# Down projection of a ConvFFN: low parts of weight operands by accumulating DMAs instead of subtractions

## The chip, the cores and the metric

One core of a Trainium2 chip runs the whole block as one program. The time is device microseconds of one execution, given as the median of several runs. Three runs of the kernel before took 1481.59, 1489.31 and 1491.31 us: median 1489.31. The profile shows one execution, whose span from the first to the last instruction is 1485.7 us. In it the granted TensorE clock was 0.992 on the mean.

Engine names as in the profile: PE is TensorE's matmul (PEld its weight load), DVE VectorE, ACT ScalarE, POOL GpSimd, SP SyncE, which here only issues DMAs. Each engine works through its own queue in order. A DMA issue that has to wait holds up all that stands behind it in that queue.

## The reference

```python
def _conv_ffn(xn, w_up, conv_w, conv_b, w_down):
    hid = xn @ w_up
    hp = jnp.pad(hid, ((0, 0), (CONV_WIDTH - 1, 0), (0, 0)))
    conv = conv_b + sum(hp[:, j:j + seq_len] * conv_w[j] for j in range(CONV_WIDTH))
    val, gate = jnp.split(conv, 2, axis=-1)
    return (jax.nn.silu(gate) * val) @ w_down
...
    h = h + _conv_ffn(rmsnorm(h, norm_ffn_g), w_ffn_up, ffn_conv_w, ffn_conv_b, w_ffn_down)
    h = rmsnorm(h, norm_final_g)
    return h[:, N_META:]
```

Ahead of this stand a normalization, a forgetting attention beside a state-space model, and an output projection. The sizes: 1024 tokens and 16 meta tokens, width 1024, hidden width 2816, everything float32. The change touches only the last matrix product, the 1024x2816 by 2816x1024 down projection `@ w_down`, whose result is added to `h` and normalized.

## The kernel before

**Two-term operands.** Every float32 matrix operand is split into a high part `hi` (the value cast to fp32r, TensorE's reduced form of float32) and a low part `lo = x - hi`. A product is three matmuls: hi by hi, hi by lo, lo by hi (lines 1365, 1366, 1367 for the down projection: `ah` is the high part of the activation, `bh` and `bl` the high and the low part of the weight).

**Seven products.** The down projection is a Strassen-like scheme: both matrices are cut into 2x2 blocks, and seven products p = 0 to 6 of sums of blocks replace eight. `ORDER` takes them as 0, 4, 1, 2, 5, 3, 6. The hidden width is cut into 11 pairs of 128-row blocks, j = 0 to 10, in four groups: j = 0, 1; 2 to 4; 5 to 7; 8 to 10. A product of a group is 4 token tiles by 2 or 3 values of j by 3 matmuls of 128x128 by 128x512, gathered in four PSUM banks. Products 4, 5, 6 go on in the banks of products 0, 1, 3 (`JOINS`). Each time a bank is complete, DVE (ACT for some of the first group) adds it to the running sums in SBUF (line 1375 and lines 1370, 1373); that is called the eviction here. PE can't write on in a joined bank before its eviction has read it.

**Operand forms.** For each (group, product, j), `forms` (line 1289) makes one slot of four 128x512 tiles: activation hi and lo, weight hi and lo. There are 77 of them, numbered here in the order of the program, n = 0 to 13 in the first group, 14 to 34 in the second, and so on. For one form:

- SP loads the weight block `b_` (256 KB) into a buffer `wr` (8 buffers, line 1293): for products 0, 4 and 6 it is a block of `w_dn` itself, for 1, 2, 3 and 5 a sum of blocks that earlier DMAs have put into DRAM tensors `t_d`.
- POOL makes the activation sums in place (lines 1298 to 1304) from tiles `ar` that SP loads from `a_d`.
- ACT casts the activation and the weight to hi (line 1310).
- Both lo parts are subtractions, `split_lo` (line 129): on POOL for products 0, 4 and 5, on DVE for 1, 2, 3 and 6.

**Slots.** There are 14: four `op` tiles, eight in what `xhi` and `xlo` held before, and two more `op` tiles. Form n uses slot n modulo 14 (from the fifth on), so a slot is refilled as soon as the product that used it last has ended; `prepare` (line 1406) makes forms as far ahead as slots are free. The trace names the slots only as `op`, `xhi` and `xlo`.

**Order of the work.** The program is written in the order of `prepare` and `product`, and a scheduler of the framework then orders each engine's queue by a timing model of its own, so a changed instruction can also move its neighbours.

**The other way to make a low part**, already in the kernel, is used in the mixer's gate weights and the output projection (`lo_by_dma`, line 133): ACT writes -hi into the lo tile (line 135), then POOL issues a DMA that reads the same source block from DRAM a second time and adds it into the lo tile (line 136).

Of the kernel before, what the change touches and what calls it, by code (L numbers as in the profile page):

```python
# [19 lines left out]
P = 128  # L20
# [30 lines left out]
def block_kernel(ctx, tc, x, meta, g1, x0t, g1t, w_q, w_k, w_v, w_f, w_u, w_g, b_f, w_ao, lam_d, bw_d, cw_d,  # L51
# [5 lines left out]
    V, S, GP, PE, SY = nc.vector, nc.scalar, nc.gpsimd, nc.tensor, nc.sync  # L57
# [52 lines left out]
    t_d = {p: dp.tile([DFF // 2, 512], F, name=f"t_d{p}") for p in (1, 2, 3, 5)}  # L110
# [13 lines left out]
    def after(inst, first):  # L124
        tc.add_manual_dep(inst.ins, first.ins.name, mybir.DependencyInfo(
            mybir.DependencyClass.NoSync, mybir.DependencyReason.DATA), reason="order")

    def split_lo(eng, out_, src, hi):
        return eng.tensor_tensor(out_, src, hi.bitcast(F), ALU.subtract)  # L129
# [3 lines left out]
    def lo_by_dma(lo, hi, src):  # L133

        S.activation(lo, hi.bitcast(F), AF.Copy, scale=-1.0)
        GP.dma_start(lo, src.bitcast(R), accum_op=ALU.add)
# [784 lines left out]
    own_w = {0: (0, 0), 4: (1, 0), 6: (1, 1)}  # L921
# [277 lines left out]
    def w_block(k, h_, j):  # L1199
        c0 = P * (2 * j + k)  # L1200
        return w_dn[c0:c0 + P, 512 * h_:512 * h_ + 512]
# [76 lines left out]
    def behind(ld, j):  # L1278
        if h_load and j in groups[1]:
            after(ld, h_load[-1])  # L1280
# [9 lines left out]
    def forms(p, j):  # L1290
        r = pairs[j]
        b_ = down1.tile([P, 512], F, tag="w", name="wr", bufs=8)
        behind(SY.dma_start(b_, w_block(*own_w[p], j) if p in own_w else t_d[p][P * j:P * j + P]), j)

        a11, a21, a12, a22 = (r[k, h_] for k in range(2) for h_ in range(2))
        sub, add = ALU.subtract, ALU.add
        if p == 1:
            GP.tensor_tensor(a11, a11, a21, sub)
        elif p == 2:
            GP.tensor_tensor(a11, a22, a11, add)  # L1300
        elif p == 3:
            GP.tensor_tensor(a21, a22, a21, sub)
        elif p == 6:
            GP.tensor_tensor(a11, a11, a12, sub)
        slot = ops[n_op[0] % len(ops)]
        n_op[0] += 1
        a_ = (a11, a11, a11, a21, a12, a22, a11)[p]
        eng = GP if p in (0, 4, 5) else V
        for q, src in ((0, a_), (2, b_)):
            hi = S.copy(slot[q], src)  # L1310
            if first_copy and j < 2 and p >= 5:
                after(hi, first_copy[1])
            cut = split_lo(eng, slot[q + 1], src, slot[q])
            if first_add and eng is V and j < 2 and p > 2:
                after(cut, first_add[1 if p == 3 else 3])
        return slot
# [88 lines left out]
    def prepare():  # L1405

        while len(ready) < (len(items) if first_add else 3) and room[0] >= len(groups[items[len(ready)][0]]):
            g, p = items[len(ready)]
            room[0] -= len(groups[g])
            if p == 0:  # L1410
                for j in groups[g]:
                    load_pair(j)
            ready[g, p] = [forms(p, j) for j in groups[g]]
# [4 lines left out]
    for p in ORDER[:2]:  # L1418
        room[0] -= 2
        ready[0, p] = [forms(p, j) for j in groups[0]]  # L1420
# [416 lines left out]
```

## Time and profile before

| what | value |
|---|---|
| runs | 1481.59, 1489.31, 1491.31 us |
| median of the runs | 1489.31 us |
| span of the profiled execution | 1485.7 us |
| what lies around the span, taken as median less span | 3.6 us |
| down projection on PE, first to last matmul | about 1257.1 to 1477.8 us of the span |
| DMA load of a weight block `wr` from `t_d`, 256 KB, issue to landing | 2.8 us (median of 44) |
| the same from `w_dn` | 3.8 us (median of 33) |

The time of the profiled execution isn't listed apart from its span; the three runs lie between 4.1 us under and 5.6 us over that span, so the profiled one is an ordinary execution and the median is taken for its time.

How to read the lines shown further down. A line of the groups view has: source line, engine, operation, output<-inputs, shape, count | busy us in total, mean ns of one | idle time of the engine just before them, and what ended it. A line of the timeline has: start us, length us, engine, line, operation, output<-inputs, count of merged instructions [idle time before <- releaser]. A line of the windows view has: the stretch, its length, then the busy time of PE, PEld, DVE, ACT and POOL with the number of instructions, the granted PE clock, the mean busy share of the 16 DMA engines, and GB/s. A line of the waits view says who waited for whom: total us, times, the longest. Line 129 is the helper of all subtractions: `op<-wr,op` is a weight's low part, `op<-ar,op` an activation's.

### The profile page before, as it was taken

What the parts mean: (1) busy time and instruction counts of PE and PEld (TensorE: products, weight loads), DVE (VectorE), ACT (ScalarE), POOL (GpSimd) and SP (SyncE); (2) the same over time, 40 slices, a digit from 0 to 9 for tenths busy, and PEclk for the clock granted to TensorE, in tenths of its full rate; (3) what the DMA queues carried; (4) which work ended last, traced back from release to release, by engine and by line L of the source; (5) the groups of instructions that cost most, each with busy time, mean ns of one, the idle gap of its engine ahead of it and who ended that gap; (6) DMA issues with size and microseconds to landing.
All of it is one profiled execution on the core that took longest, in us unless ns stands there. A gap on an engine that the chain in (4) does not pass through costs nothing. (4 is left out here: it accounts for less than half of the span.)

```text
span 1485.7 us, 26584 instructions
## 1 busy us (share of the span) xinstructions
PE 1440.4 (97%) x9712; PEld 1358.8 (91%) x9712; DVE 1071.4 (72%) x2173; ACT 712.2 (48%) x1384; POOL 742.1 (50%) x850
## 2 busy tenths in 40 slices
PE   7999997999999999999999999999999999998997
PEld 7989996998899999999888999999999999777886
DVE  6879648881566676647468987888877776788785
ACT  6434675541555665543546534444444445543433
POOL 1311125752456465524863144455544426789766
PEclk9999999999999999999999999999999999999999
DMA  6366571551127342047885135676653215765513
GB/s 246 86 157 157 128 163 50 177 160 43 48 79 178 93 111 90 26 148 256 257 158 185 57 109 141 178 199 188 174 143 100 84 57 180 286 203 148 168 40 114
DMA packets 91032, 206.72 MB, mean 139 GB/s; under 512 B 14651, under 2 KB 25531, under 8 KB 90517
## 3 DMA queue, kind: packets, MB, share of 16 engines
q1 hardware_dynamic: 69380, 159.73, 32.9%
q0 software_dynamic: 15296, 34.63, 13.2%
q10 hardware_dynamic: 6224, 10.65, 1.9%
q8 instruction: 77, 1.26, 0.3%
q14 instruction: 55, 0.44, 0.1%
HBM read 165.90 MB, written 69.35 MB: 158 GB/s over the span
## 5 line engine op out<-in xcount | busy, mean ns | idle before, releaser
L159 PE MATMUL mm<-xhi,whi 128*128 128x342 f32 (+2 forms) x488 | 159.4, 327 | 1.0 <-DVE q L129 1.0
L161 PE MATMUL mm<-xhi,wlo 128*128 128x342 f32 (+2 forms) x488 | 158.3, 325 | 0.0
L160 PE MATMUL mm<-xlo,whi 128*128 128x342 f32 (+2 forms) x488 | 157.7, 324 | 0.0
L1079 POOL TENSOR_TENSOR ov<-ov,og 128x1024 f32<-128x1024 f32 x21 | 51.1, 2434 | 125.6 <-ACT og L1078 121.7
L129 DVE TENSOR_TENSOR sw<-sf,sw 128x512 fp32r<-128x512 f32 x72 | 66.6, 925 | 50.0 <-ACT sw L1070 49.8
L1070 ACT CAST sw<-sf 128x512 fp32r<-128x512 f32 x72 | 44.9, 624 | 106.2 <-POOL sf L1196 74.5
L159 PEld LDWEIGHTS mm<-xhi,whi 128*128 128x128 f32 x488 | 91.9, 188 | 2.1 <-PE sp L714 0.8
L161 PEld LDWEIGHTS mm<-xhi,wlo 128*128 128x128 f32 x488 | 91.8, 188 | 0.3
L160 PEld LDWEIGHTS mm<-xlo,whi 128*128 128x128 f32 x488 | 91.9, 188 | 0.2
L763 ACT CAST th<-tp 128x256 fp32r<-128x256 f32 (+3 forms) x120 | 56.2, 472 | 62.5 <-PE tp L756 30.1
L129 DVE TENSOR_TENSOR tl<-tp,th 128x256 fp32r<-128x256 f32 (+3 forms) x120 | 65.2, 547 | 25.1 <-ACT th L763 23.7
L1196 POOL TENSOR_TENSOR sf<-raw,sf 128x512 f32<-128x512 f32 x36 | 59.1, 1641 | 44.8 <-DVE sw L129 44.7
L1196 POOL TENSOR_TENSOR sf<-raw 128x512 f32<-128x512 f32 x36 | 48.0, 1332 | 66.9 <-DMA raw<-in_w_up_dram 35.9
L221 PE MATMUL mm<-xhi,sw 128*128 128x258 f32 (+1 forms) x288 | 81.0, 281 | 0.0
L219 PE MATMUL mm<-xhi,sw 128*128 128x258 f32 (+1 forms) x288 | 80.8, 281 | 0.0
L220 PE MATMUL mm<-xlo,sw 128*128 128x258 f32 (+1 forms) x288 | 80.7, 280 | 0.0
L728 POOL TENSOR_SCALAR pt<-pt,nm 128x144 f32<-128x144 f32 (+4 forms) x72 | 51.8, 731 | 48.5 <-DVE nm L727 47.5
L1248 DVE SCALAR_TENSOR_TENSOR ov<-hv,cwt,ov 128x1024 f32<-128x1024 f32 x36 | 72.5, 2014 | 0.1
L1070 ACT CAST sw<-raw 128x512 fp32r<-128x512 f32 x70 | 43.0, 621 | 53.3 <-PE sp L221 25.5
L726 ACT ACTIVATE pt<-pt,nm 128x144 f32<-128x144 f32 (+4 forms) x72 | 52.9, 735 | 26.1 <-DVE nm L725 25.7
L719 DVE CUSTOM_DVE_ANT_0 pt<-sp,fb 128x328 f32<-128x328 f32 (+8 forms) x112 | 46.4, 430 | 20.0 <-PE sp L714 11.1
L756 PE MATMUL tp<-ident,pt 128*128 128x128 f32 (+1 forms) x360 | 58.3, 270 | 0.1
(708 smaller groups left out, 5702.1 us busy)
## 6 DMA issues: line engine op xcount, KB each, us to landing
raw<-in_w_up_dram SPq DMA_DIRECT2D x44, 512.0 KB, 3.6
t_d<-in_w_dn_dram POOLq DMA_DIRECT2D x44, 256.0 KB, 7.0
ar<-a_d SPq DMA_DIRECT2D x44, 256.0 KB, 5.1
wr<-t_d SPq DMA_DIRECT2D x44, 256.0 KB, 2.8
a_d<-ov SPq DMA_DIRECT2D x21, 512.0 KB, 2.6
wr<-in_w_dn_dram SPq DMA_DIRECT2D x33, 256.0 KB, 3.8
t_d<-in_w_dn_dram SPq DMA_DIRECT2D x22, 256.0 KB, 4.2
t_d<-t_d SPq DMA_DIRECT2D x22, 256.0 KB, 4.7
```

The source lines that it names most:

```text
L129: return eng.tensor_tensor(out_, src, hi.bitcast(F), ALU.subtract)
L159: yield PE.matmul(ps, whi[:, i, :], ahi[:, i], start=(i == 0), stop=False)
L160: yield PE.matmul(ps, whi[:, i, :], alo[:, i], start=False, stop=False)
L161: yield PE.matmul(ps, wlo[:, i, :], ahi[:, i], start=False, stop=(i == k - 1))
L219: PE.matmul(ps, a[0][:, i], bh, start=(i == 0 and not joins), stop=False, skip_group_check=True)
L220: PE.matmul(ps, a[0][:, i], bl, start=False, stop=False, skip_group_check=True)
L221: PE.matmul(ps, a[1][:, i], bh, start=False, stop=(i == kh - 1), skip_group_check=True)
L756: PE.transpose(tp[:kn, o:o + n], p_[:n, k0:k0 + kn], ident[:n, :n])
L763: S.copy(th[:kn, z:tw], tp[:kn, z:tw])
L1070: S.copy(hi, src)
L1196: sums.append(GP.tensor_tensor(f_, a, b, op))
L1248: V.scalar_tensor_tensor(out=o, in0=h_[:, j:SEQ + j], scalar=cwc(j, m), in1=o, op0=ALU.mult, op1=ALU.add)
```

## The change

In `forms`, the low part of the weight is no longer a subtraction for j >= 2, that is for the second to fourth group: `lo_by_dma` makes it. For j = 0 and 1 all stays, as do the low parts of the activations. The source of the weight block gets a name, so that both the load and the accumulating DMA can use it.

```diff
     def forms(p, j):
         r = pairs[j]
         b_ = down1.tile([P, 512], F, tag="w", name="wr", bufs=8)
-        behind(SY.dma_start(b_, w_block(*own_w[p], j) if p in own_w else t_d[p][P * j:P * j + P]), j)
+        b_src = w_block(*own_w[p], j) if p in own_w else t_d[p][P * j:P * j + P]
+        behind(SY.dma_start(b_, b_src), j)
...
         eng = GP if p in (0, 4, 5) else V
         for q, src in ((0, a_), (2, b_)):
             hi = S.copy(slot[q], src)
+            if q and j >= 2:
+                lo_by_dma(slot[3], slot[2], b_src)
+                continue
             if first_copy and j < 2 and p >= 5:
                 after(hi, first_copy[1])
             cut = split_lo(eng, slot[q + 1], src, slot[q])
```

The function that it calls, as it stands in both kernels:

```python
    def lo_by_dma(lo, hi, src):

        S.activation(lo, hi.bitcast(F), AF.Copy, scale=-1.0)
        GP.dma_start(lo, src.bitcast(R), accum_op=ALU.add)
```

The build shows that no queue is reordered ahead of the down projection. In the queues of the down projection 36 subtractions leave DVE and 27 leave POOL; 63 copies with scale -1 join ACT's queue, and 63 DMA issues join POOL's. On PE the number of matmuls stays, and around the change from the first to the second group their order is another.

## The prediction

> **What bounds the kernel now.** I read the page's head first, then the windows view over the down projection, then PE's waits there.
>
> ```profile
> span 1485.7 us, 26584 instructions
> PE 1440.4 (97%) x9712; PEld 1358.8 (91%) x9712; DVE 1071.4 (72%) x2173; ACT 712.2 (48%) x1384; POOL 742.1 (50%) x850
> ...
> 1257.00:1478.00 221.00, 212.43 (x935) 173.55 (x933) 175.10 (x214) 96.96 (x190) 176.46 (x127) 1.00 0.49 156
> 1265.00:1335.00 70.00, 67.91 (x297) 55.29 (x297) 54.26 (x61) 36.99 (x69) 58.57 (x39) 1.00 0.75 252
> 1265.00:1445.00 180.00, 173.57 (x758) 141.43 (x758) 146.31 (x169) 81.51 (x154) 148.34 (x103) 1.00 0.56 174
> ```
>
> PE is the bound: in the 221 us of the down projection it is busy for 212.43 us at full clock, so it stands idle for 8.57 us. The change doesn't touch a matmul, so 8.57 us is all that it can win in this stretch. DVE and POOL are busy for 175 us each and ACT for 97; none is the bound, but each can hold PE up. The idle time, from the waits of PE in the same stage:
>
> ```profile
> PE mm L1365 <- ACT xlo L1310: 3.0, 1, 3.0
> PE tp L1365 <- DVE hs L1375: 2.7, 2, 2.0
> PE mm L1365 <- DVE hs L1375: 1.1, 1, 1.1
> PE sp L1367 <- POOL op L129: 0.9, 1, 0.9
> PE sp L1365 <- DVE hs L1375: 0.6, 1, 0.6
> ```
>
> The 1.1 us (a load of `hs`) and 2.0 of the 2.7 us (the last product) have nothing to do with weights. The 3.0 us ended at 1368.6; here is DVE ahead of it:
>
> ```profile
> 1357.52 3.48 DVE L129 TENSOR_TENSOR op<-wr,op 128x512 fp32r<-128x512 f32 x2
> 1360.92 2.33 DVE L129 TENSOR_TENSOR op<-ar,op 128x512 fp32r<-128x512 f32 x1
> ...
> 1366.58 0.68 DVE L129 TENSOR_TENSOR xhi<-wr,xhi 128x512 fp32r<-128x512 f32 x1
> 1367.18 0.68 DVE L1375 TENSOR_TENSOR hs<-hs,tp 128x512 f32<-128x512 f32 x1
> 1367.77 1.87 DVE L1375 TENSOR_TENSOR u<-u,mm 128x512 f32<-128x512 f32 x3
> ```
>
> The eviction of the joined `mm` bank starts at 1367.77, and one of it takes 0.6 us: PE goes on at 1368.6. The wait is put down to ACT, but the eviction fits it better; it stood behind three weight subtractions.
>
> **What the change removes.** The groups of the stage, weight subtractions on both engines:
>
> ```profile
> L129 POOL TENSOR_TENSOR op<-wr,op 128x512 fp32r<-128x512 f32 x19 | 27.6, 1465 | 0.0
> L129 DVE TENSOR_TENSOR op<-wr,op 128x512 fp32r<-128x512 f32 x15 | 22.7, 1520 | 0.0
> L129 DVE TENSOR_TENSOR xhi<-wr,xhi 128x512 fp32r<-128x512 f32 x15 | 16.9, 1130 | 0.0
> L129 DVE TENSOR_TENSOR xlo<-wr,xlo 128x512 fp32r<-128x512 f32 x14 | 15.9, 1144 | 0.0
> L129 POOL TENSOR_TENSOR xhi<-wr,xhi 128x512 fp32r<-128x512 f32 x8 | 12.6, 1578 | 0.0
> L129 POOL TENSOR_TENSOR xlo<-wr,xlo 128x512 fp32r<-128x512 f32 x6 | 8.6, 1439 | 0.0
> ```
>
> DVE: 44 in 55.5 us, 1.26 us each; 8 of the first group stay, 36 go: 45 us. POOL: 33 in 48.8 us, 1.48 us each; 6 stay, 27 go: 40 us. Neither is on PE's path as such. What DVE's 45 us are worth is the evictions that stand behind them: 3.0 + 0.6 + 0.7 us = 4.3 us. Bounds: 0 (another activation subtraction takes the place in the queue) and 4.3; I take 4.3, because in the changed order of DVE the evictions of a bank follow each other with fewer subtractions between them. The 0.9 us of PE on POOL goes as well, since that place is priced anew below.
>
> **What it adds.** The same construction stands in the output projection; its rows:
>
> ```profile
> L135 ACT ACTIVATE op<-op x8: 615/625/636, 719.6 to 755.1; 128x512 fp32r<-128x512 f32 x8
> ...
> L136 POOL DMA_DIRECT2D op<-to_d x4: 877/1293/1795, 724.1 to 725.8; - x4
> ...
> DMA to landing us min/median/max: 4.1/6.8/12.1
> ...
> op<-to_d POOLq DMA_DIRECT2D x4, 256.0 KB, 9.9
> ...
> 724.08 3.54 POOL L136 DMA_DIRECT2D op<-to_d  x4
> 726.40 1.49 POOL L129 TENSOR_TENSOR mstk<-md,mstk 128x24 fp32r<-128x24 f32 x1
> ...
> 747.00:753.00 6.00, 6.00 (x29) 4.93 (x28) 2.59 (x5) 3.68 (x8) 2.72 (x5) 1.00 1.12 214
> 1275.00:1290.00 15.00, 15.00 (x68) 12.43 (x67) 14.35 (x17) 8.39 (x16) 12.08 (x8) 1.00 1.05 390
> ```
>
> ACT: 63 x 0.625 = 39 us, which makes 97 into 136 of 221 us: cover enough, price 0. SP: its loads of weights wait for buffers that the subtractions hold:
>
> ```profile
> SPq L1293 <- POOL op L129: 43.0, 17, 10.2
> ```
>
> A buffer is now free after ACT's cast, so these loads start sooner and price 0 is safe; what comes late next is the DMA engines, which then have loads and accumulations at once. POOL: the row of an issue is 1.29 us long, but four of them let the next work start 2.32 us after the first, so one holds POOL for 0.58 us: 63 x 0.58 = 37 us against 40 removed. POOL stays where it was; if an issue holds it for the whole 1.29 us, 81 us come and POOL stands at 218 of 221 (a rival below). Behind an issue that waits for ACT's copy, or for the landing of the eighth DMA before it, stand the activation sums; eight in 9.9 us are 1.24 us each, and only one every 2.9 us (221 us by 77 forms) is needed, so that wait is covered. DMA engines: while nearly only such transfers ran (747 to 753) they moved 214 GB/s at a full share, against 390 GB/s for plain loads (1275 to 1290). One of 256 KB is thus 1.22 us of all engines, 63 are 77 us. Between 1265 and 1445 the share is 0.56 of 180 us = 101 us; 178 of 180 are used then, or of 202 if the last operands may come until 1467. That is full, but not over, as long as transfers start early.
>
> **Where latency counts.** A subtraction ends 1.3 to 1.8 us after POOL gets to it, a DMA lands 4.1 to 12.1 us after its issue. How much sooner than needed were the low parts ready? Late in the stage:
>
> ```profile
> 1429.00 1.74 POOL L129 TENSOR_TENSOR op<-wr,op 128x512 fp32r<-128x512 f32 x1
> ...
> 1450.67 0.39 PE L1365 MATMUL mm<-op 128*128 128x512 f32 x1
> ```
>
> The last weight of product 5 of the fourth group is ready at 1430.7 and its product begins at 1450.67: 20 us. Such slack covers even 12.1 us; price 0. At the start of the second group there is none:
>
> ```profile
> 1290.07 1.75 POOL L1300 TENSOR_TENSOR ar<-ar 128x512 f32<-128x512 f32 x1
> 1291.78 3.00 POOL L129 TENSOR_TENSOR op<-wr,op 128x512 fp32r<-128x512 f32 x2
> 1294.74 1.75 POOL L1302 TENSOR_TENSOR ar<-ar 128x512 f32<-128x512 f32 x1
> 1296.45 3.54 POOL L129 TENSOR_TENSOR op<-wr,op 128x512 fp32r<-128x512 f32 x2
> 1299.95 1.74 POOL L1300 TENSOR_TENSOR ar<-ar 128x512 f32<-128x512 f32 x1
> ...
> 1294.87 0.39 PE L1366 MATMUL sp<-op 128*128 128x512 f32 x1
> ```
>
> Form 14, the group's first, is subtracted from 1291.78 to 1293.3, and PE uses it at 1294.87. In the changed queue of POOL nine operations precede the DMA of form 14, as many as before, so it is issued at about 1291.8. Form 15 follows two sums later (0.58 + 1.75 + 1.74: 1295.9), 16 at once (1296.5), 17 after a subtraction (1298.6), 18 and 19 after a sum (1300.9, 1301.5). PE's changed order does 16 more matmuls, 0.23 us each, ahead of form 14: wanted at 1298.5; then 12 matmuls to form 15 (1301.2) and 12 to form 16 (1303.9), 8 to 17 (1305.7), 8 to 18 (1307.5), 13 to 19 (1310.5). With the median landing of 6.8 us form 15 is the latest: 1302.7, 1.5 us late. With 9.9 it lands at 1305.8, 4.6 us late, and no later form is later than that. With 4.1 none is late, with 12.1 it is 6.8 us. The DMA engines are full until 1290, as they were when the 9.9 was measured, so I take 4.6.
>
> The Trainium skill (page "DMA: Bandwidth & Descriptors", section "Anatomy of one DMA — SWDGE (gpsimd) path") gives 2.0 us plus bytes/436e3 for a DMA issued from GpSimd, by estimate 2.6 us for 256 KB. The trace doesn't agree for accumulating ones: 4.1 us is the least of 29. By the page no form would be late, and the sum would be -5.2 us.
>
> **The sum** against the profiled execution, for which I take the median (span + 3.6 us): -0.9 (POOL wait) - 4.3 (evictions) + 4.6 (form 15) = -0.6 us: 1488.7. Ends: -5.2 us (1484.1) with landings of 4.1 us; with landings of 12.1 us and no eviction gained -0.9 + 6.8 = +5.9 us (1495.2). What ends last is not moved: the last product's operands are ready 20 us before it, as above.
>
> **Rivals.** (a) *Slower: the DMA engines become the bound of the second group.* From 1265 to 1335 they are busy for 0.75 x 70 = 52.5 us; 21 accumulating transfers add 25.6: 78 us in 70. Then loads and accumulations of that group are 8 us late on top of form 15's 4.6: 1489.3 + 12.6 = 1502. It decides if PE consumes the second group faster than this; for it speaks the share of 1.05 around 1280, against it that part of these loads are the next group's, which have time: the share falls again by itself. If an accumulation shares the engines with loads and so takes twice as long, 51 us come and it may be 1510. (b) *Slower: POOL becomes the bound*, with 1.29 us an issue: 21 issues hold the activation sums of the second group up by 21 x 0.71 = 15 us: 1504. Against it is the pitch of 0.58 us. The skill (page "SBUF — State Buffer", section "SBUF: two separate sides") warns that GpSimd can't write descriptors while DVE runs in a two-port mode, which would be such a hold. (c) *A gain of all that can go*, -5.2 us and up to -5.5: 1484; for it speak the landings of 4.1 us, against it the burst's 9.9. (d) *Nothing seen*, because evictions still wait and form 15 is in time: 1489, in the forecast's own range.
>
> **How the numbers follow.** About 1% (14.9 us) is what a measurement of this kernel can tell from no change. Forecast with (d), 1488.7, own range 1484 to 1495: 0.56. (c): 0.2, all within 1%. (a): 0.18, over half of it beyond 1504.2. (b): 0.06, half beyond. A gain over 1% would need more than PE's idle time: 0.03 for runs that scatter (the three differ by 9.7 us). Slower by over 1%: 0.16; within 1%: 0.81; faster: 0.03. The range from 1481 to 1505 reaches below (c) by the scatter of the runs and above to (a) and half of (b).
>
> **What would show it.** Right: 36 and 27 subtractions gone, PE's waits on evictions near 1348 to 1369 gone, a new wait of PE on a DMA near 1298 to 1306 of a few us, POOL at about 173 us between 1257 and 1478, DMA share near 0.95 from 1265 to 1445, and low parts of the last two groups landing ten us or more ahead of PE. Wrong: PE idle more than 15 us in the stage, in many places (a), POOL without a gap and ACT waiting for its sums (b).

## The result, and the profile after

The changed kernel takes 1503.06 us (median of 4 runs, 1502.19 to 1505.14) against 1487.01 us of the kernel before in the same comparison (1481.59 to 1491.31): a ratio of 1.0102, 95% interval 1.0079 to 1.0125. The forecast was no change, 1488.7 us; the result is slower, at the place that the prediction gave to its rival (a), 1502 us. The profiled execution took 1503.0 us.

The down projection from its first to its last matmul in the kernel before, by the windows view (columns as in the prediction's rows):

```profile
1257.11:1477.84 220.73, 212.32 (x935) 173.44 (x933) 174.86 (x213) 96.69 (x190) 176.46 (x127) 1.00 0.49 156
```

The head of the page of the changed kernel:

```profile
span 1501.2 us, 26676 instructions
PE 1445.3 (96%) x9712; PEld 1362.1 (91%) x9712; DVE 1053.9 (70%) x2137; ACT 745.6 (50%) x1447; POOL 747.9 (50%) x886
```

Its windows view, first the same stage from first to last matmul, then the prediction's stretches and two around long stalls:

```profile
1253.39:1493.86 240.47, 220.43 (x935) 179.74 (x933) 158.35 (x177) 130.72 (x254) 180.99 (x163) 0.95 0.84 213
1265.00:1335.00 70.00, 65.05 (x272) 52.57 (x271) 44.40 (x49) 44.72 (x84) 55.53 (x49) 0.95 1.06 304
1265.00:1445.00 180.00, 162.07 (x675) 131.48 (x674) 119.11 (x117) 104.05 (x195) 142.80 (x130) 0.93 1.00 253
1345.00:1365.00 20.00, 14.82 (x55) 11.71 (x54) 18.16 (x15) 9.96 (x20) 20.00 (x21) 0.83 0.91 207
1405.00:1425.00 20.00, 12.20 (x50) 9.73 (x49) 14.61 (x8) 13.70 (x27) 20.00 (x20) 0.80 0.86 197
```

The stage grew from 220.73 to 240.47 us, by 19.7 us (it began 3.7 us sooner, which the work ahead of it does from run to run: over the profiles below it begins between 1253.4 and 1259.8). PE idles for 20.04 us in place of 8.41, which is 11.6 us; and its busy time is 8.1 us longer for the same 935 matmul records, at a granted clock of 0.95 on the mean: it was 1.00 over the stage before, and is 0.83 and 0.80 in the two 20 us windows that hold long stalls. The DMA engines are full, 1.00 from 1265 to 1445 us, where the prediction's row of the kernel before had 0.56. Who made PE wait, from the waits view of the stage:

```profile
PE mm L1369 <- DVE hs L1379: 12.7, 3, 7.8
PE tp L1369 <- DVE hs L1379: 7.3, 2, 5.2
```

Five waits, all on evictions (line 1379 now), none on a DMA. The three new ones lie at the start of each changed group: 3.64 us at 1298.06, 5.18 at 1356.59 and 7.80 at 1422.55. Behind each of them the clock is halved for 4 to 6 us, and matmuls begin 0.43 us apart in place of 0.23; behind the wait of 3.0 us in the kernel before it isn't. First the three places, then that one:

```profile
1298.00:1304.00 6.00, 5.94 (x13) 4.40 (x14) 1.20 (x3) 2.14 (x5) 6.00 (x8) 0.50 1.10 262
1356.00:1362.00 6.00, 5.41 (x13) 4.25 (x14) 6.00 (x6) 0.62 (x1) 6.00 (x8) 0.50 0.91 174
1422.00:1426.00 4.00, 3.45 (x8) 2.80 (x9) 4.00 (x5) 2.71 (x5) 4.00 (x5) 0.50 0.92 242
1368.00:1374.00 6.00, 5.41 (x24) 4.45 (x25) 6.00 (x7) 1.07 (x3) 6.00 (x5) 1.00 1.06 240
```

The last of the three waits, followed back in the timeline of the changed kernel (start, length, instruction, idle time before it):

```profile
1402.88 0.62 ACT L1311 CAST op<-ar 128x512 fp32r<-128x512 f32 x1 [11.40 <-DMA ar<-a_d]
...
1403.59 1.29 POOL L129 TENSOR_TENSOR op<-ar,op 128x512 fp32r<-128x512 f32 x1 [10.94 <-ACT op L1311]
1404.85 1.29 POOL L1299 TENSOR_TENSOR ar<-ar 128x512 f32<-128x512 f32 x1
1406.09 1.75 POOL L136 DMA_DIRECT2D op<-in_w_dn_dram  x2
1407.23 1.93 POOL L1299 TENSOR_TENSOR ar<-ar 128x512 f32<-128x512 f32 x1
1408.49 1.91 POOL L1303 TENSOR_TENSOR ar<-ar 128x512 f32<-128x512 f32 x1
1409.75 3.14 POOL L129 TENSOR_TENSOR op<-ar,op 128x512 fp32r<-128x512 f32 x2
...
1411.36 10.45 DVE L129 TENSOR_TENSOR xhi<-ar,xhi 128x512 fp32r<-128x512 f32 x2 [4.04 <-ACT xhi L1311]
1421.73 1.87 DVE L1379 TENSOR_TENSOR hs<-hs,mm 128x512 f32<-128x512 f32 x3
...
1422.55 0.76 PE L1369 MATMUL mm<-xlo 128*128 128x512 f32 x1 [7.80 <-DVE hs L1379]
```

An activation load `ar` comes late: ACT stands for 11.40 us, and POOL behind it for 10.94. Then POOL catches up without a pause; its first DMA issues come at 1406.09, and from there each operation begins before the record of the one ahead of it has ended (1407.23 + 1.93 is after 1408.49). In that stretch two subtractions of DVE, 0.68 us each when nothing is beside them, take 10.45 us. The eviction that PE needs stands behind them. So there are two suspects, late loads and held-up subtractions, and the experiments set them against each other.

Late loads, by the DMA issues of the changed kernel's stage (KB each, median us to landing):

```profile
ar<-a_d SPq DMA_DIRECT2D x36, 256.0 KB, 7.2
wr<-t_d SPq DMA_DIRECT2D x36, 256.0 KB, 5.9
wr<-in_w_dn_dram SPq DMA_DIRECT2D x28, 256.0 KB, 8.2
op<-t_d POOLq DMA_DIRECT2D x17, 256.0 KB, 11.9
```

Before, the first three were 5.4, 2.8 and 3.7 us. The medians hide the loads that count. The landings of all `ar` loads of the stage, and ACT's waits for them, each time before and then after:

```profile
DMA to landing us min/median/max: 2.6/5.4/7.7
DMA to landing us min/median/max: 4.0/7.2/16.3
ACT op L1310 <- DMA ar<-a_d: 2.7, 2, 2.2
ACT xlo L1310 <- DMA ar<-a_d: 3.7, 2, 1.9
ACT op L1311 <- DMA ar<-a_d: 14.4, 3, 11.4
ACT xlo L1311 <- DMA ar<-a_d: 12.0, 2, 10.4
```

The wait of 10.4 us ends at 1337.3, ahead of PE's second new wait, and that of 11.4 us at 1402.9, ahead of the third. No such wait stands ahead of the first.

### The profile page after: what moved, and what is told of

Same layout as the page of the kernel before. It is cut to its first block, busy times and chain, and to the rows that moved or that the text cites. A ratio compares the mean times of both kernels' runs of the same rounds, so it can differ in the third digit from the quotient of the medians.

```text
span 1501.2 us, 26676 instructions
## 1 busy us (share of the span) xinstructions
PE 1445.3 (96%) x9712; PEld 1362.1 (91%) x9712; DVE 1053.9 (70%) x2137; ACT 745.6 (50%) x1447; POOL 747.9 (50%) x886
## 3 DMA queue, kind: packets, MB, share of 16 engines
q8 instruction: 76, 1.25, 0.3%
## 4 chain that ended last, share of the span: by engine, by line
PE 80%; DVE 8%; DMA 5%; issue 3%; ACT 2%; POOL 1%; SPq 1%; ACTq 0%; POOLq 0%; DVEq 0%
PE mm L161 5%; PE mm L159 5%; PE mm L160 5%; PE sp L219 4%; PE sp L220 4%; PE sp L221 4%; PE tp L219 3%; PE tp L220 3%; PE tp L221 3%; PE mm L221 3%; PE mm L219 3%; PE mm L220 3%; PE tp L756 2%; DMA ar<-a_d 2%; PE po L778 2%
```

## The experiments

Each kernel was compared with the kernel before on the same chip; times are medians, ratios are to the kernel before with their 95% interval. The expectations set theory B (bytes: full DMA engines make loads and low parts late) against theory P (port: DVE's subtractions stand still while POOL works without a gap behind its DMA issues, and the evictions stand behind them).

### Fewer bytes

**e1_cols64.** The issues stay, 7/8 of the bytes go.

```diff
-                lo_by_dma(slot[3], slot[2], b_src)
+                S.activation(slot[3], slot[2].bitcast(F), AF.Copy, scale=-1.0)
+                GP.dma_start(slot[3][:, :64], b_src[:, :64].bitcast(R), accum_op=ALU.add)
```

> The changed kernel, but each accumulating DMA moves 64 of the 512 columns; the other columns of the low parts are left as minus the high parts (this leaves the source out of 7/8 of the low parts). Issues, waits and orders stay, 7/8 of the accumulated bytes go. Theory P (port): single DVE subtractions of 4 to 6.5 us, which stand still while POOL's work runs without a gap behind DMA issues, hold the evictions up; the bytes don't matter: 1503 us, with DVE subtractions of over 4 us and PE waits of 3 to 8 us on evictions still there. Theory B (bytes): the 16 DMA engines, at a share of 0.93 to 1.11, make loads and low parts late: 1484 to 1489 us, no such waits.

Measured: 1487.31 us, ratio 0.9988 (0.9976 to 0.9999). The loss is gone, so the bytes carry it: theory P as the only cause falls. But its rows are not gone: two DVE subtractions still take 3.21 us (at 1292.37) and 4.06 us (at 1296.10), and PE still waits 3.6 us for an eviction right behind them. That is the first of the changed kernel's three new waits; the other two, of 5.18 and 7.80 us, are gone, and ACT waits for no `ar` load longer than 2.4 us. The subtractions that the change removed are gone here as well, and yet hardly anything is won.

**e5_cols256.** The same lines with `:256` in place of `:64`.

> The changed kernel with 256 of the 512 columns accumulated (the source is left out of half of the low parts). DMA engines: busy 131 us of the stage with 64 columns and 202 us with 512, so some 161 us by bytes, 0.73 of the stage. Theory T (threshold: loads are late only where the engines are full): 1487 to 1490 us. Theory L (every byte costs its share): 1487 + 16 x 3/7 = 1494 us.

Measured: 1489.41 us, ratio 1.0005 (0.9990 to 1.0020), a DMA share of 0.72 in the stage. From 64 to 256 columns costs 0.17%, some 2.5 us, from 256 to 512 costs 0.97%, some 14 us: a threshold (T), not a price per byte (L).

**e6_plain_write.** The DMA writes, it doesn't add.

```diff
+                S.activation(slot[3], slot[2].bitcast(F), AF.Copy, scale=-1.0)
+                GP.dma_start(slot[3], b_src.bitcast(R))
```

> The changed kernel with the 63 DMAs of POOL as plain copies of the same 256 KB (nothing is subtracted: the low parts are the sources). At the 390 GB/s of plain loads 63 take 42 us of all engines instead of 77. If what fills the engines is that an accumulation takes nearly twice a copy's time: share 0.68 of the stage, loads in time, 1487 to 1491 us. If the number of packets and queues matters and not the kind: 1500 to 1505 us.

Measured: 1482.28 us, ratio 0.9967 (0.9953 to 0.9980), below the range expected. With as many bytes landing the engines are busy for 0.74 x 217.35 = 161 us of the stage; the kernel before has 0.49 x 220.73 = 108, the changed one 0.84 x 240.47 = 202. A plain 256 KB thus took (161 - 108) / 63 = 0.84 us of all engines, an accumulating one (202 - 108) / 63 = 1.49 us. The landings in the traces say the same: beside the loads, the changed kernel's low parts land 2.00 us apart (22 of them from 1298.5 to 1340.7), the plain copies mostly 1.36 us apart.

The run also shows what full engines alone don't do. From 1285 to 1325 us their share is 1.13 here, and the stage's median loads land nearly as late as in the changed kernel (6.6 us for `ar`, 5.7 and 5.9 us for `wr`, against 7.2, 5.9 and 8.2). But no `ar` takes over 10.4 us, ACT waits for none longer than 2.3 us, and nothing is lost.

### One group at a time

**e9_group2_only, e10_groups34, e8_group4_only.** The condition `if q and j >= 2` becomes `2 <= j < 5`, `j >= 5` and `j >= 8`.

> The changed kernel with DMAs in the second group alone (21). From 1265 to 1335 us the engines were busy for 52.5 us; 21 accumulations at the 1.5 to 1.7 us that the stages with 63 and 21 of them give are 32 to 36 us more, 84 to 88 in 70 us: full there, with room after it. Rival (a) of the prediction (the second group alone carries the loss): 1498 to 1503 us. Theory T with a backlog that builds up over all groups: 1487 to 1491 us, with the one PE wait of about 3.6 us near 1298 that every variant with issues in this group has.

Measured: 1498.94 us, ratio 1.0072 (1.0052 to 1.0092). The second group alone brings two thirds of the loss, as rival (a) had it. The windows of this kernel:

```profile
1305.00:1345.00 40.00, 40.00 (x168) 32.70 (x168) 17.12 (x22) 18.09 (x34) 29.32 (x29) 0.95 1.07 267
1345.00:1385.00 40.00, 31.70 (x130) 25.51 (x129) 39.34 (x34) 14.00 (x26) 37.57 (x29) 0.87 0.68 170
```

Its longest wait of PE, and the longest subtraction in DVE's timeline:

```profile
PE mm L1369 <- DVE u L1379: 8.3, 1, 8.3
```

```profile
1369.74 7.95 DVE L129 TENSOR_TENSOR xhi<-wr,xhi 128x512 fp32r<-128x512 f32 x1
```

Most of the loss doesn't fall in the second group, though, where PE waits 3.7 us: the engines stay full until 1345, the third group's first `ar` loads are late by it (ACT waits 9.3 us for one), POOL catches up, and PE's long wait of 8.3 us follows at 1379 behind a subtraction of 7.95 us. The only DMAs that POOL issues there are the four of `hs<-h_d`, from 1362 to 1370, which the kernel before has too.

> The changed kernel with DMAs in the third and fourth group (42). Busy 108 + 42 x 1.5 to 1.7 = 171 to 179 of 221 us, a share of 0.77 to 0.81, between the 0.72 that cost nothing and the 0.84 that cost 16 us. Theory T: no ACT wait on a load over 6 us; 1483 to 1489 us, without the wait of 3 us that the kernel before has near 1368. If the engines are full locally from 1345 to 1425 (109 us of work in 80) and that is enough: 1492 to 1500 us.

Measured: 1495.49 us, ratio 1.0054 (1.0034 to 1.0073): the share over the whole stage, 0.77, hid it; over the 80 us from 1345 to 1425 it was 0.97. PE waits 3.5 us on an eviction and 3.6 us on a low part itself (`op<-t_d`).

> The changed kernel with DMAs in the fourth group alone (21 instead of 63). In the kernel before the DMA engines have room there. If full engines are the root: loads in time, no long catch-up of POOL, 1484 to 1489 us. If the issues alone hold DVE up at the start of a group: one stall of 4 to 8 us with the lower clock after it, 1492 to 1496 us.

Measured: 1486.47 us, ratio 0.9989 (0.9975 to 1.0002). Where the engines have room (0.31 before from 1385 to 1425) 21 accumulations cost nothing that can be seen, and bring nothing.

### POOL beside DVE

**e2_act_on_dve.** POOL only issues, DVE does the activations' sums and subtractions.

```diff
-            GP.tensor_tensor(a11, a11, a21, sub)
+            (V if j >= 2 else GP).tensor_tensor(a11, a11, a21, sub)
...
-        eng = GP if p in (0, 4, 5) else V
+        eng = GP if p in (0, 4, 5) and j < 2 else V
```

> The changed kernel, with the activations' sums and subtractions of the second to fourth group all on DVE; POOL only issues DMAs there. Theory P: no POOL operation reads SBUF beside DVE, so every DVE subtraction takes 0.68 us, PE's waits on evictions are at most those of before, 1482 to 1489 us. Theory B: DMA traffic is the same, 1503 us.

Measured: 1493.58 us, ratio 1.0038 (1.0026 to 1.0050), between the two theories. No DVE subtraction took over 0.69 us, as P has it; but ACT still waits for loads and DVE's sums and subtractions wait with it. PE's longest wait, 5.9 us for an eviction at 1311.9, stands behind weight loads that ACT waits for (up to 3.2 us each); the longest wait for an `ar`, 12.8 us until 1400.5, is followed by 3.8 us of PE on ACT at 1414.8.

**e14_dve_64.** Both edits at once, e2_act_on_dve with 64 columns.

> The activations' sums and subtractions all on DVE (as in the kernel of 1493.6 us) and 64 of the 512 columns accumulated (the source is left out of 7/8 of the low parts). Neither bytes nor POOL operations beside DVE. If the 6 us of the kernel with all bytes are late loads that hold sums, and so evictions, up on DVE: they go, 1482 to 1488 us. If it is the longer queue of DVE itself: 1491 to 1495 us.

Measured: 1478.92 us, ratio 0.9939 (0.9921 to 0.9957), below the range of its first case. That completes a table of ratios; its last row has no accumulating DMA for these low parts, and its right-hand kernel (e18_all_dve) follows further down:

| | activation work on POOL and DVE | on DVE alone |
|---|---|---|
| 512 columns accumulated | 1.0102 (the change) | 1.0038 |
| 64 columns | 0.9988 | 0.9939 |
| all subtracted | 1 (the kernel before) | 0.9946, weights on DVE too |

The bytes cost 1.14% and 0.99% (17 and 15 us), POOL's operations beside DVE's cost 0.64% and 0.49% (9 and 7 us), whichever way the other is set. Within their intervals (some 0.2% each) the two costs add. But the second isn't a cost of the change: the last row has it as well, 0.54% (8 us), without the 63 issues. The kernel before already pays it. From the kernel before to the change there are then 2 us less (to 0.9988, subtractions gone and issues added) and 17 us more (the bytes).

**e13_no_dve_sub.** All DMAs and POOL's queue as in the change; ACT takes the place of DVE.

```diff
+            if j >= 2 and eng is V:
+                S.activation(slot[q + 1], src, AF.Copy, scale=2.0 ** -12)
+                continue
             cut = split_lo(eng, slot[q + 1], src, slot[q])
```

> The changed kernel, but the activations' low parts of products 1, 2, 3 and 6 in the second to fourth group are made by a scaling copy on ACT in place of the subtraction on DVE (36 operations of 0.62 us, ACT some 153 us of the stage; half of the activations' low parts are then wrong in value). POOL's queue and all 63 DMAs stay. If the loss goes by way of starved DVE subtractions: evictions have nothing slow ahead of them, no PE wait on an eviction over 2.2 us, 1486 to 1493 us. If late loads alone make it: 1500 to 1505 us, with PE waiting on operands.

Measured: 1495.55 us, ratio 1.0046 (1.0027 to 1.0065), just above the range of the first theory. With nothing slow on DVE some 8 us are won back (1.0102 to 1.0046): half of the loss passes through DVE's subtractions. ACT still waits 13.7 us for an `ar`, and the other half shows its own face now, a late low part:

```profile
PE sp L1373 <- DMA op<-t_d: 9.2, 1, 9.2
```

**e4_tiny_issues.** The kernel before, with 63 DMAs of next to no bytes on POOL.

```diff
+        if j >= 2:
+            tiny = down1.tile([P, 16], F, tag="tiny", name="tiny", bufs=8)
+            GP.dma_start(tiny, b_src[:, :16])
         return slot
```

> The kernel before, with every subtraction kept, and one further DMA of 64 bytes a partition (16 columns of the weight block, into a tile that nobody reads) issued by POOL for each of the 63 forms of the second to fourth group. Theory P: the issues alone make POOL's work close up and DVE's subtractions stand still: 1493 to 1505 us, with single DVE subtractions of over 3 us. Theory B: the bytes are 2 MB and POOL has 37 us more, so 1487 to 1490 us and DVE subtractions of at most 1.8 us.

Measured: 1514.45 us, ratio 1.0175 (1.0158 to 1.0193): far slower, above even the range of P, with hardly any bytes (63 times 8 KB are 0.5 MB, not the 2 MB expected). Its timeline, POOL and then DVE:

```profile
1319.24 0.56 POOL L1319 DMA_DIRECT2D tiny<-t_d  x1
1319.82 1.30 POOL L129 TENSOR_TENSOR op<-ar,op 128x512 fp32r<-128x512 f32 x1
1321.07 1.30 POOL L129 TENSOR_TENSOR op<-wr,op 128x512 fp32r<-128x512 f32 x1
1322.33 1.28 POOL L1303 TENSOR_TENSOR ar<-ar 128x512 f32<-128x512 f32 x1
1323.58 1.26 POOL L1299 TENSOR_TENSOR ar<-ar 128x512 f32<-128x512 f32 x1
1325.47 1.68 POOL L1301 TENSOR_TENSOR ar<-ar 128x512 f32<-128x512 f32 x1 [0.63 <-DVE xhi L129]
...
1319.90 5.49 DVE L129 TENSOR_TENSOR xhi<-ar,xhi 128x512 fp32r<-128x512 f32 x1
```

Behind an issue four operations of POOL follow each other every 1.25 us, and DVE's subtraction, which began with the first, ends at 1325.39: only when POOL stands idle at 1324.84 does it get its 0.6 us. In the kernel before, from 1290 to 1300 us, POOL's operations mostly came 1.5 to 1.7 us apart, with about one subtraction of DVE to each. POOL has 197 us of work in this stage against 176 before, so the run doesn't tell how much of the 26 us is held subtractions and how much POOL's longer queue.

**e7_tiny_memsets** was to tell the issue from any other short work of POOL.

```diff
-            GP.dma_start(tiny, b_src[:, :16])
+            GP.memset(tiny, 0.0)
```

> The kernel before with 63 memsets of 16 columns on POOL where the 1514 us kernel had tiny DMA issues: POOL work of about the same length (0.5 us), but no DMA. Theory P (after a DMA issue POOL's operations follow each other without letting DVE's subtractions in until POOL stands idle): 1487 to 1494 us and DVE subtractions of at most 2 us. Rival (POOL simply has 30 us too much to do): 1510 to 1516 us, as with the issues.

Measured: 1488.46 us, ratio 1.0010 (0.9997 to 1.0023). The number agrees with P, but the experiment failed to ask its question: the memsets wait for nothing, so they ran in one row ahead of the stage, from 1231 to 1244 us, and took 0.11 us each.

**e15_no_h_issues** is the better control: the kernel before without the only DMAs that POOL issues in its down projection.

```diff
-            if g == 1 and p == 3:
-                GP.dma_start(bot, h_d[P * (4 + t):P * (4 + t) + P], accum_op=ALU.add)
```

> The kernel before without the four accumulating DMAs hs<-h_d that POOL issues from 1358.7 to 1363 (the residual is left out of the lower half of the output). If these issues are why DVE's subtractions take 3.48 (two) and 2.33 us there: at most 1.78 us each then, PE's wait of 3.0 us near 1368 is gone or under 1.5 us, 1484 to 1487 us. If the weight subtractions ahead of the eviction are enough for that wait, as the prediction had it: it stays at 2.5 to 3.5 us, 1487 to 1489 us.

Measured: 1486.92 us, ratio 0.9983 (0.9969 to 0.9997). The subtraction of 2.33 us is 1.78 us now, and PE's wait of 3.0 us is 1.5 us: half of that wait goes with these four DMAs (issues and 2 MB of bytes, not told apart), the other half stays with the subtractions. (The row of 3.48 us stays; it holds two of 1.74 us.) All subtractions on DVE in this kernel, from 1265 us on, by the view of line 129 (shortest/median/longest in ns, first to last start), where POOL works for 173.9 us of the stage but issues nothing:

```profile
L129 DVE TENSOR_TENSOR op<-ar,op x15: 680/1276/1787, 1275.5 to 1431.2; 128x512 fp32r<-128x512 f32 x15
```

and in the changed kernel:

```profile
L129 DVE TENSOR_TENSOR op<-ar,op x15: 681/1592/6537, 1274.5 to 1449.2; 128x512 fp32r<-128x512 f32 x15
L129 DVE TENSOR_TENSOR xhi<-ar,xhi x11: 677/1121/5741, 1282.9 to 1456.8; 128x512 fp32r<-128x512 f32 x11
```

The longest single subtraction thus sorts the kernels: 1.79 us beside POOL's operations without issues (80 subtractions in e15_no_h_issues); 0.69 us beside issues without POOL's operations (e2_act_on_dve, e14_dve_64); and 4.06 to 13.11 us in the seven kernels that have both in the second group (the changed one, e1_cols64, e4_tiny_issues, e5_cols256, e6_plain_write, e9_group2_only, e11_dve_products). With both from the third group on it is 3.95 us in e10_groups34 and 10.15 in e12_dve_products_34. Both together are not enough, though: e8_group4_only has them in the fourth group, and no subtraction there takes over 2.18 us.

**e3_act_on_pool** went the other way, with `eng = GP if p in (0, 4, 5) or j >= 2 else V`.

> The changed kernel, with the activations' subtractions of the second to fourth group all on POOL; DVE only evicts there (one operand in PSUM, one in SBUF). POOL then has 111 operations of 1.25 us and 63 issues of 0.58 us, 175 of 221 us. Theory P: evictions take 0.68 us each with nothing slow ahead of them; 1485 to 1490 us, unless POOL itself falls behind, which would show as PE waiting on POOL's subtractions and not on evictions. Theory B: 1503 us with the same waits as in the changed kernel.

Measured: 1534.90 us, ratio 1.0310 (1.0293 to 1.0328), a miss for both theories. PE waits on ACT's casts (20.6 us in five waits) and on low parts (5.3 us in three), little on evictions. POOL has work for 221.6 us of a stage of 259.6, and ACT waits 16.4 us for an `ar`; the run doesn't tell the two suspects apart.

### Fewer DMAs

**e11_dve_products, e12_dve_products_34.** Only the products whose weights DVE subtracted are changed: `if q and j >= 2 and p in (1, 2, 3, 6)`, then the same with `j >= 5`.

> The changed kernel with DMAs only for the products whose subtractions ran on DVE (1, 2, 3 and 6; 36 DMAs); POOL keeps its 27 weight subtractions. DMA engines 108 + 36 x 1.5 to 1.7 = 162 to 169 us, 0.73 to 0.77 of the stage: by theory T no late loads. POOL has 176 + 36 x 0.58 = 197 us of 221. 1484 to 1490 us if POOL keeps up; 1495 to 1510 us if POOL's issues make it late and hold DVE up, as the tiny issues did (1514 us with 63).

Measured: 1503.87 us, ratio 1.0113 (1.0094 to 1.0133). 36 DMAs lose as much as 63, at a share of 0.68. POOL now has 196 us of work with issues in it, and at the worst place no load is late; PE waits 6.5 us there, until 1318.3:

```profile
1304.56 13.11 DVE L129 TENSOR_TENSOR op<-ar,op 128x512 fp32r<-128x512 f32 x1 [0.83 <-ACT op L1311]
1317.60 0.67 DVE L1379 TENSOR_TENSOR u<-u,tp 128x512 f32<-128x512 f32 x1
```

> The same as the kernel with the DVE products alone, in the third and fourth group only (24 DMAs). 108 + 24 x 1.6 = 146 us of DMA engines, 0.66; POOL 190 of 221 us. If the evictions behind DVE's weight subtractions are worth the 4.3 us of the prediction and nothing else stands in the way: 1482 to 1485 us. If issues beside POOL's subtractions hold DVE up: 1488 to 1495 us.

Measured: 1496.89 us, ratio 1.0060 (1.0044 to 1.0076), just above its second case; two subtractions in a row take 11.82 us at 1369.22.

Neither run is free of late loads: ACT waits 12.8 us for an `ar` until 1402.1 in the first and 10.1 us until 1399.8 in the second. That wait sorts nearly all the kernels of this document. The longest one for an `ar` is 9.3 to 16.4 us in the eight that accumulate whole tiles in the second or third group (the changed one, e2, e3, e9, e10, e11, e12, e13), and all eight are slower than the kernel before. It is at most 4.7 us in the kernel before and in ten others, none of them slower beyond its interval. Only e4_tiny_issues is slow without it (5.2 us).

### Kernels that keep both costs out

**e16_half_256, e17_half_128.** On top of e2_act_on_dve, each low part is split (n = 256, then 128).

```diff
+                n = 256
+                S.activation(slot[3][:, :n], slot[2][:, :n].bitcast(F), AF.Copy, scale=-1.0)
+                GP.dma_start(slot[3][:, :n], b_src[:, :n].bitcast(R), accum_op=ALU.add)
+                split_lo(V, slot[3][:, n:], b_[:, n:], slot[2][:, n:])
```

> Activation work of the second to fourth group on DVE, POOL only issues; of each low part of the weights 256 columns by accumulating DMA and 256 by a subtraction on DVE. All is computed. DMA share about 0.72 as with 256 columns before, DVE 155 + 63 x 0.36 = 177 us. If full engines and POOL operations beside DVE are the two costs: 1478 to 1485 us, faster than both kernels. If 0.72 of the engines or the longer queue of DVE makes evictions late: 1487 to 1492 us.

Measured: 1480.44 us, ratio 0.9944 (0.9928 to 0.9960).

> The same with 128 columns by DMA and 384 on DVE: DMA share about 0.65, DVE 155 + 63 x 0.5 = 187 us of 216. If the DMA engines are the tighter of the two: a little faster than with 256 columns, 1478 to 1484 us. If DVE is: slower, 1484 to 1490 us.

Measured: 1481.46 us, ratio 0.9953 (0.9940 to 0.9967), not told apart from the one above.

**e18_all_dve.** The kernel before with the edit of e2_act_on_dve alone, and no DMA for a low part.

> The kernel before with the activations' sums and all subtractions of the second to fourth group on DVE; no accumulating DMA for weights, POOL nearly idle there. DVE 155 + 63 x 0.62 = 194 us of 220. If it is enough to keep POOL's operations away from DVE: 1478 to 1485 us, and the DMAs have no part in the gain. If DVE's queue is then too long: 1488 to 1500 us.

Measured: 1480.92 us, ratio 0.9946 (0.9931 to 0.9961). This is the simplest version that beats both kernels, and it shows that the DMAs have no part in the gain. Its groups on DVE, then all its waits of PE in the stage:

```profile
L129 DVE TENSOR_TENSOR op<-ar,op 128x512 fp32r<-128x512 f32 x30 | 20.6, 688 | 0.9 <-ACT op L1310 0.5 <-PE tp L1366 0.4
L129 DVE TENSOR_TENSOR op<-wr,op 128x512 fp32r<-128x512 f32 x30 | 20.4, 688 | 0.0
```

```profile
PE tp L1365 <- DVE hs L1375: 2.1, 1, 2.1
PE mm L1365 <- DVE hs L1375: 1.3, 1, 1.3
```

A subtraction takes 688 ns on the mean, where DVE's `op<-wr,op` took 1520 and POOL's 1465 before. DVE does its own work and POOL's in 185.4 us of a stage of 215.13, about the 174.9 us that it was busy before. The profile accounts for 5.6 us of a shorter stage; the ratio says 8 us with an interval of 5.8 to 10.3, and where the rest lies isn't settled.

## Why the prediction was wrong, point by point

- **The DMA engines, "full, but not over", price 0: this step failed.** The engines were full from 1265 to 1445 us as forecast (1.00, against 178 of 180 us). The bytes cost 15 to 17 us (the table). Two things were missing. An accumulation took 1.49 us of all engines and not 1.22: from 1265 to 1445 that makes 101 + 94 = 195 us of work for 180. The prediction's own row said part of it: it had 214 GB/s at a share of 1.12, not 1, which makes 1.37 us of all engines and 187 us, over and not full. And what comes late is not only a low part: `ar` loads take up to 16.3 us to land in place of 7.7, and the one that a group begins with holds ACT, POOL and DVE up in turn. The sum over the stage hid this: e9_group2_only loses 10 us with 21 DMAs at a mean share of 0.59, since the engines stood at 1.07 from 1305 to 1345 us. Rival (a) had this sum for 1265 to 1335 us, with a chance of 0.18. Its mechanism was right in the cause; the place of the longer waits is one group later. That its 1502 us lies 1 us from the result is partly luck: the 4.6 us of form 15 in it were not seen, and its 8 us would be 14 with 1.49 us for an accumulation. Its second size, accumulations that take twice as long beside loads (51 us for 21), was nearer to the landings: 42 us, at 2.00 us each.
- **POOL, "stays where it was", price 0: the term was right and the question wrong.** POOL's busy time went from 176.46 to 173.04 us between 1257 and 1478 (180.99 over the longer stage), and two issues in a row still begin 0.6 us apart. What the issues did to DVE wasn't priced: subtractions of up to 6.54 us, 2.33 before, and PE's first new wait of 3.64 us, which e1_cols64 has too. Its share of the time isn't isolated. Rival (b) looked at this meeting from the wrong end: it had POOL held by DVE, and the runs show DVE held by POOL.
- **The eviction gain of 4.3 us.** It is there to be had (PE idle 4.9 us in e14_dve_64 and 3.4 in e18_all_dve, 8.4 before), but those kernels win it by taking POOL's operations off DVE's way, not by this change. The evictions stood behind subtractions that were slow because POOL worked beside them (0.69 us with that work moved), and half of the 3.0 us goes with four DMAs of POOL (e15_no_h_issues). The rows were quoted in the prediction: 2.33 us for one subtraction, beside the mean of 1.26 us that it reckoned with for DVE, was the sign that was passed over. With POOL's issues added, the remaining subtractions got slower and the evictions later. With the DVE weight subtractions gone and an eighth of the bytes (e1_cols64), gain and loss nearly cancel.
- **Form 15 late by 4.6 us: not seen.** In the changed kernel PE waits for no DMA at all, since its evictions are later than its operands. The landing times were sized about right (medians of 6.5 to 12.2 us by tile and source, against a forecast of 4.1 to 12.1). When the evictions are made early, a low part is late, by 9.2 us, in the third group and not the second (e13_no_dve_sub). The 20 us of slack that the fourth group had did not hold for the third.
- **Price 0 for ACT and for SP's loads.** ACT's added 34 us cost nothing that shows. The loads did not start early enough to matter: SP now waits for ACT's casts (23.0 us on `xhi` alone), which wait for loads themselves.
- **The clock** was no term of the sum. In the change it made about 8 of the stage's 19.7 us, as longer matmuls after the stalls.

By the measured terms, in shares of 1487 us: -2 us (e1_cols64: subtractions gone, issues added) + 17 (the bytes) = +15 us, against 16.05 us between the medians. That they meet is no test, since both terms are differences of the same ratios. The trace gives one of its own: PE's two waits that e1_cols64 doesn't have are 5.18 + 7.80 = 13 us, and the matmuls at half clock behind them add some 5 us, by estimate from their pitch of 0.43 us: 18 us, near the 17 of the bytes.

Of the signs that were listed ahead, "PE idle more than 15 us in the stage, in many places (a)" came true as to its length, with 20.0 us in five places; the DMA share of 0.95 was 1.00; PE's waits on evictions from 1348 to 1369 did not go but grew to 5.18 us; the wait on a DMA near 1298 to 1306 did not come: the 3.64 us at 1298.06 was an eviction.

**Still open.** Why POOL's operations leave DVE no turn once POOL has issued a DMA, until POOL stands idle, isn't shown; only that it is so in the timelines of the second and third group (and not in the fourth of e8_group4_only), and that without issues no subtraction took over 1.8 us. Whether other short work on POOL does the same wasn't tried with success. And a held subtraction costs only if an eviction that PE needs stands behind it: in e6_plain_write one took 6.48 us and PE idled for only 4.5 us in the whole stage, so part of each variant's loss may be where its queue happens to put things. In e11_dve_products a held subtraction and a late load both stand ahead of waits, and how the loss divides between them is open.

## What to carry to other kernels

Price a DMA edit in the stretch where the engines are fullest, with the duration of its own kind beside the loads that share the engines, and ask which load the next stage begins with and when it lands. A share over 1 is neither free nor a price by itself: 1.07 for 60 us cost 10 us in e9_group2_only, 1.13 for 40 us nothing in e6_plain_write. Before work is taken off VectorE, see what makes it slow: a subtraction of two SBUF tiles took 0.69 us alone, up to 1.8 us beside GpSimd work, and up to 13 us where GpSimd also issued DMAs. Moving all such work to VectorE and leaving GpSimd nearly idle won 0.5% here; moving the weights' part of it to DMAs lost 1%. When one record of a kind is much longer than its neighbours, look at what the other engines issue in that moment.

## What the runs showed of the hardware

- Subtractions of DVE with both inputs in SBUF were held for up to 13.11 us, through several operations of POOL (e11_dve_products); 128x512 evictions, with one input in PSUM, took 0.67 to 0.69 us each in that kernel, also right behind them.
- The Trainium skill (page "SBUF — State Buffer", section "SBUF: two separate sides") says that a VectorE operation with two SBUF inputs and a GpSimd operation that reads SBUF exclude each other, and that whoever starts first has the port for its whole instruction. The trace agrees as to who is held (0.69 us beside issues alone, 0.67 to 0.69 for evictions); it differs as to how long, since 13.11 us is not one instruction of POOL, whose pitch is 1.25 us.
- While both kinds of transfers ran at a share of 1.00 the engines moved 253 GB/s, between the 214 GB/s of accumulations and the 390 of plain loads. Over the whole stage, 256 KB took 1.49 us of all engines as an accumulation and 0.84 as a plain copy on the same queue.
- After PE's waits of 3.64, 5.18 and 7.80 us the granted clock was 0.50 for 4 to 6 us (0.83 and 0.80 over the 20 us around the last two); after one of 3.0 us in the kernel before it was 1.00.
